# A gate table built in pipelined steps of four tokens, with projection weights split ahead and pick indices stored in pairs

## The chip, the core and the metric

The kernel runs on one core of one Trainium2 chip. A core has five engines that run at the same time: TensorE (PE in the profile; its weight loads are PEld), VectorE (DVE), ScalarE (ACT), GpSimd (POOL) and SyncE (SP, which issues DMA transfers). The metric is the device time of one execution in microseconds, the median of several runs.

## What is computed

The reference is one decoder block on 1024 tokens of width 1024: a mixing sub-layer (a short convolution beside windowed attention) and a retrieval of experts. In the retrieval each token has 8 heads; each head scores 128 "a" keys and 128 "b" keys, keeps the 16 best of each, adds them pairwise, keeps the 16 best sums and so names 16 of 16384 experts:

```python
q = (ht @ wq).reshape(t, PEER_HEADS, 2, PEER_DK)
va, ia = lax.top_k(sa, PEER_TOPK)
vb, ib = lax.top_k(sb, PEER_TOPK)
...
top, pos = lax.top_k(cand, PEER_TOPK)
eidx = jnp.take_along_axis(cidx, pos, axis=-1)
g = jax.nn.softmax(top, axis=-1).astype(ht.dtype)
a = jax.nn.gelu(jnp.einsum('thkd,td->thk', u, ht))
return jnp.einsum('thk,thkd->td', g * a, v)
```

## The kernel before

**Stages.** Three "fronts" treat 384, 384 and 256 tokens. A front does 18 input projections (`w_in`), attention and convolution, 8 output projections (`w_out`), and 16 query projections (`wq`) whose scores go through a first top 16. By the instructions of lines 342 to 560 in the trace, the first front runs to about 343 us, the second from 343 to 729, the third from 729 to 1023. Then `dense` follows: every expert against tokens 0 to 639, on TensorE, to the end. Tokens 640 to 1023 fetch their experts by indirect DMA beside it.

**Projections.** `proj` multiplies one 128-column block of weights in two half chunks of 4 x 128 rows. For a half chunk SyncE loads `wraw`, ScalarE makes `wH` (L268), GpSimd makes the remainder `wL` (L269, 128x512, both inputs in SBUF), and TensorE runs 12 matmuls (L272).

**The gate table.** The dense stage needs, for each token, a 128x128 table with the gate g at (ia, ib). For a block of 128 tokens `select` (L593 to L671) picks the 128 (ia, ib, g) triples of each token, and `spread` (L683 to L717) turns them around with three transposes, so that a token's 128 triples lie on the 128 partitions, and builds one table per token as a matmul of two one-hot matrices: `oi`, a row of g at column ia, and `oj`, a row of 1 at column ib. It works in steps of four tokens. The four `oi` of a step are made one by one, by the letters of `HOT = "APVV"`: one by ScalarE in two activations (L703, L704), one by GpSimd and two by VectorE (L706, a compare with `iota` times g, 128x128). VectorE makes `oj` for all four at once (L711, 128x512, two inputs in SBUF). TensorE does four matmuls into one PSUM tile `gps` (L714), ScalarE copies it out (L715), and a DMA writes 32 tokens' tables to `gd`. Five blocks (tokens 0 to 639) go through `spread`: 160 steps.

**Order.** `select` and `spread` are generators. They advance in `bg`, which `proj` calls once at its start with a credit that comes to about 4 steps for 384 tokens and 3 for 256. So blocks 0 to 2 are spread within the second front and blocks 3 and 4 within the third. The framework's scheduler then orders each engine's instructions; an engine runs its own queue strictly in that order, and semaphores hold an instruction until its inputs and its buffer are free.

**Picking.** In `select`, L660 makes a one-hot over 16 ranks (128x2048, bf16), L662 multiplies it by the candidates' indices `idf`, which are broadcast along the innermost dimension, and L666 and L668 add up.

Of the kernel before, what the change touches and what calls it, by code (L numbers as in the profile page):

```python
# [47 lines left out]
GT = 3  # L48
J = 4
TB = 32  # L50
HOT = "APVV"
RATE0, RATE = 0.0, 0.49
ORDER = True
BACK = 0
# [20 lines left out]
def hymba_peer_kernel(ctx: ExitStack, tc: tile.TileContext, a, out: bass.AP):  # L75
# [181 lines left out]
    def ch(t, c):  # L257
        return t[c // 4][:, c % 4, :]

    def proj(wsrc, sH, sL, T):  # L260
        bg(24 * T / 2400 + 0.5)
        pt = pj.tile([P, TM], F32, name="pj")
        for h in range(2):
            w = wp.tile([P, 4, P], F32, name="wraw")
            nc.sync.dma_start(w, wsrc[:, 4 * h:4 * h + 4, :])
            wH = wp.tile([P, 4, P], F32R, name="wH")
            wL = wp.tile([P, 4, P], F32R, name="wL")
            A.copy(wH, w)  # L268
            G.tensor_tensor(wL, w, wH.bitcast(F32), op=ALU.subtract)  # L269
# [62 lines left out]
    def front(t0, T, hs, nxt):  # L332
# [9 lines left out]
        A.copy(kc, proj(a["w_in"][4], hH, hL, T))  # L342
        qT = [tmp("y", bufs=4)[:, 0:T] for c in range(4)]
        for c in range(4):
            A.copy(qT[c], proj(a["w_in"][c], hH, hL, T))
        vT = tmp("q")
        A.copy(vT[:, 0:T], proj(a["w_in"][5], hH, hL, T))

        def conv():
            ys = []  # L350
            for cc in range(4):
                cs = tmp("q")[:, 0:T]
                A.copy(cs, proj(a["w_in"][6 + 3 * cc], hH, hL, T))
# [3 lines left out]
                V.tensor_tensor(u[:, 2:T + 2], cs, proj(a["w_in"][7 + 3 * cc], hH, hL, T), op=ALU.mult)  # L357
# [6 lines left out]
                V.tensor_tensor(y, y, proj(a["w_in"][8 + 3 * cc], hH, hL, T), op=ALU.mult)  # L364
# [191 lines left out]
        for mm in range(0, 16, 2):  # L556
            qs = []
            for m in (mm, mm + 1):
                qq = tmp("q")[:, 0:T]
                A.copy(qq, proj(a["wq"][m], h2H, h2L, T))  # L560
# [30 lines left out]
            V.max_index(u[:, 8:16], v[:, 8:16], s)  # L591

    def select(va, iu):  # L593
        idf = sel.tile([P, 2 * PH, 16], BF16, name="idf")
        A.copy(idf, iu)
        va4 = va.rearrange("p (h s) k -> p h s k", s=2)
        id4 = idf.rearrange("p (h s) k -> p h s k", s=2)
        cand = sel.tile([P, PH, NCAND], F32, name="cand")
# [7 lines left out]
        pairs(1, 3, 8, 16)  # L606
        pairs(4, 4, 4, 40)
        pairs(8, 8, 1, 56)
        top = sel.tile([P, PH, 16], F32, name="top")
        pu = sel.tile([P, PH, 16], U32, name="pu")  # L610
        yield
        for m0 in range(0, 8, 4):
# [44 lines left out]
        for s, src in ((0, aab), (1, stb)):  # L657
            r = ft(f"pick{s}", tag=("a3", "st3")[s])
            hot1 = sel.tile([P, PH, 16, 16], BF16, name="hot1")
            V.tensor_tensor(hot1, src.rearrange("p (h k) -> p h k", h=PH).unsqueeze(2).to_broadcast([P, PH, 16, 16]),  # L660
                            rank.unsqueeze(1).to_broadcast([P, PH, 16, 16]), op=ALU.is_equal)
            V.tensor_tensor(hot1, hot1, id4[:, :, s, :].unsqueeze(3).to_broadcast([P, PH, 16, 16]), op=ALU.mult)  # L662
            yield
            m = 8
            while m > 1:
                V.tensor_tensor(hot1[:, :, 0:m, :], hot1[:, :, 0:m, :], hot1[:, :, m:2 * m, :], op=ALU.add)  # L666
                m //= 2
            V.tensor_tensor(r.rearrange("p (h k) -> p h k", h=PH), hot1[:, :, 0, :], hot1[:, :, 1, :], op=ALU.add)  # L668
            yield
            res.append(r)  # L670
# [10 lines left out]
        V.tensor_copy(gate[:, ti, :], g)  # L681

    def spread(ti, ia, ib, g):  # L683
        gb = env["gb"]
        pat = HOT
# [3 lines left out]
        tr = gb.tile([P, 3, P], F32, name="tr", bufs=2)  # L689
        A.copy(tr, tps)  # L690
        ng = gb.tile([P, 2, P], F32, name="ng", bufs=1)
        A.activation(ng, tps[:, 0:3:2, :], AF.Copy, scale=-1.0)
        for q in range(P // TB):
            stage = gat.tile([P, P, TB], F32, name="stage")
            for t4 in range(0, TB, 4):
                ps = gp.tile([P, 4, P], F32, name="gps")
                ois = []
                for x in range(4):
                    t = q * TB + t4 + x
                    oi = gb.tile([P, P], F32, name="oi", bufs=6)  # L700
                    who = pat[t % len(pat)]
# [6 lines left out]
                    ois.append(oi)  # L708
                t = q * TB + t4
                oj = gb.tile([P, 4, P], F32, name="oj", bufs=2)  # L710
                V.tensor_tensor(oj, iota.unsqueeze(1).to_broadcast([P, 4, P]),  # L711
                                tr[:, 1, t:t + 4].unsqueeze(2).to_broadcast([P, 4, P]), op=ALU.is_equal)
                for x in range(4):
                    PE.matmul(ps[:, x, :], ois[x], oj[:, x, :], start=True, stop=True)  # L714
                A.copy(stage[:, :, t4:t4 + 4], ps.rearrange("p t j -> p j t"))  # L715
                yield
            nc.sync.dma_start(gd[(ti * P - DT0) // TB + q], stage)  # L717

    def gather():
        state = {"n": 0}  # L720
# [299 lines left out]
    with tc.tile_pool(name="ada", bufs=2, side="right") as ap:  # L1020
# [109 lines left out]
```

## Time and profile before

| | us |
|---|---|
| median of 3 runs | 2851.67 (2851.33 to 2851.88) |
| the profiled execution | 2857.49 |
| its span, first to last instruction | 2855.7 |
| VectorE busy in the span | 2373.4 (83%) |
| TensorE busy | 2700.5 (95%) |
| GpSimd busy | 1721.7 (60%) |
| ScalarE busy | 1093.9 (38%) |

The shares are means over stages that differ. The time of a stage is read from the rows of that stage. A busy TensorE is not TensorE at its peak, since its matmuls overlap.

### The profile page before, as it was taken

The page shows a single profiled execution, that of the slowest core. Times are in us where ns is not written, and L with a number is a line of the kernel's source. Part 1 is how long each engine was busy: PE and PEld are TensorE (multiplying, and loading weights), DVE is VectorE, ACT ScalarE, POOL GpSimd, SP SyncE. Part 2 cuts the span into 40 slices and gives each one's busy share as a digit, 9 for nine tenths or more (in the row PEclk, how much of TensorE's full clock was granted, in tenths as well). Part 3 has the DMA queues.
Part 4 walks back from the last instruction along what each step waited for, and adds up shares of the span by engine and source line. Part 5 has one row for each costly group of instructions (what it writes and reads, how often), then busy time and mean ns, then how long its engine had stood idle before and what let it go on. Part 6 is the DMA issues. An engine that isn't in the chain of part 4 may idle for free.

```text
span 2855.7 us, 45148 instructions
## 1 busy us (share of the span) xinstructions
PE 2700.5 (95%) x15679; PEld 2445.9 (86%) x15679; DVE 2373.4 (83%) x4845; ACT 1093.9 (38%) x2193; POOL 1721.7 (60%) x1491
## 2 busy tenths in 40 slices
PE   8899988999787889999999999999999999999998
PEld 6788978789786778889989989999989889988987
DVE  3665898877899697888988888888889888888887
ACT  2455468775586643222322222232222222222221
POOL 3444475656667744666666666666666666666661
PEclk7999999999999989999999999999999999999999
DMA  7647423464344677999999999999999999999995
GB/s 243 217 155 232 121 103 115 158 216 156 97 151 137 234 227 229 342 337 343 326 322 346 340 344 335 349 325 332 347 334 324 325 339 346 333 336 345 324 327 193
DMA packets 345157, 764.31 MB, mean 268 GB/s; under 512 B 31296, under 2 KB 130016, under 8 KB 341984
## 3 DMA queue, kind: packets, MB, share of 16 engines
q0 software_dynamic: 112320, 408.99, 39.6%
q1 hardware_dynamic: 231168, 349.81, 37.4%
q8 instruction: 123, 2.02, 0.3%
q10 hardware_dynamic: 1440, 2.62, 0.2%
q14 instruction: 106, 0.87, 0.1%
HBM read 702.06 MB, written 59.24 MB: 267 GB/s over the span
## 4 chain that ended last, share of the span: by engine, by line
PE 44%; DMA 8%; DVE 6%; issue 5%; POOL 2%; ACT 1%; SPq 0%; DVEq 0%; POOLq 0%; ACTq 0%
PE pv L873 22%; PE pa L816 21%; DMA vraw<-in_v 4%; DMA uraw<-in_uT 2%; DVE pq L768 2%; DVE vdL L860 1%; POOL rows L741 1%; ACT vdH L859 1%; DVE rows L760 1%; DMA wraw<-in_wq 1%; DMA rows<-in_v,eidx 1%; POOL uL L800 1%; DVE dacc L892 0%; DVE gw L835 0%; PE pj L272 0%
## 5 line engine op out<-in xcount | busy, mean ns | idle before, releaser
L816 PE MATMUL pa<-h,uH 128*128 128x320 f32 x4096 | 772.9, 311 | 15.2 <-ACT uH L799 6.2
L816 PEld LDWEIGHTS pa<-h,uH 128*128 128x128 f32 x4096 | 648.8, 189 | 23.1 <-ACT uH L799 7.2
L873 PE MATMUL pv<-vdH,wdH 128*128 128x512 f32 x1275 | 500.0, 392 | 18.0 <-DVE dacc L892 16.4
L269 POOL TENSOR_TENSOR wL<-wraw,wH 128x512 fp32r<-128x512 f32 x252 | 351.5, 1402 | 272.7 <-ACT wH L268 249.4
L873 PE MATMUL pv<-vdL,wdH 128*128 128x512 f32 x1275 | 497.8, 390 | 0.1
L873 PE MATMUL pv<-vdH,wdL 128*128 128x512 f32 x1275 | 496.8, 390 | 0.0
L816 PE MATMUL pa<-h,uL 128*128 128x320 f32 x2048 | 469.2, 310 | 2.3 <-POOL uL L800 2.3
L800 POOL TENSOR_TENSOR uL<-uraw,uH 128x512 fp32r<-128x512 f32 x256 | 342.4, 1338 | 163.3 <-ACT uH L799 142.7
L741 POOL DMA_INDIRECT rows<-in_u,eidx x257 | 260.8, 1015 | 157.1 <-DVE aw L760 83.2
L741 POOL DMA_INDIRECT rows<-in_v,eidx x254 | 253.7, 999 | 164.6 <-DVE pq L768 117.1
L816 PEld LDWEIGHTS pa<-h,uL 128*128 128x128 f32 x2048 | 344.6, 189 | 3.3 <-POOL uL L800 3.3
L768 DVE SCALAR_TENSOR_TENSOR pq<-rows,aw,pq 128x1024 f32<-128x1024 f32 x253 | 324.5, 1282 | 3.3 <-DMA rows<-in_v,eidx 0.8
L892 DVE TENSOR_TENSOR dacc<-dacc,pv 128x512 f32<-128x512 f32 x310 | 211.9, 684 | 134.0 <-PE pv L873 111.4
L859 ACT CAST vdH<-vraw 128x512 fp32r<-128x512 f32 x255 | 153.5, 619 | 439.0 <-DMA vraw<-in_v 366.4
L799 ACT CAST uH<-uraw 128x512 fp32r<-128x512 f32 x256 | 158.3, 619 | 418.9 <-DMA uraw<-in_uT 340.5
L760 DVE CUSTOM_DVE_ANT_0 rows<-rows,pq 128x1024 f32<-128x1024 f32 x257 | 307.5, 1212 | 12.5 <-DMA rows<-in_u,eidx 10.9
L873 PEld LDWEIGHTS pv<-vdH,wdH 128*128 128x128 f32 x1275 | 239.6, 188 | 74.9 <-DVE dacc L892 24.7
L873 PEld LDWEIGHTS pv<-vdH,wdL 128*128 128x128 f32 x1275 | 239.8, 188 | 50.9
L873 PEld LDWEIGHTS pv<-vdL,wdH 128*128 128x128 f32 x1275 | 239.8, 188 | 47.3 <-DVE vdL L860 0.5
L706 POOL TENSOR_SCALAR oi<-iota,tr 128x128 f32<-128x128 f32 x160 | 198.5, 1243 | 96.2 <-PE gps L714 88.1
L860 DVE TENSOR_TENSOR vdL<-vraw,vdH 128x512 fp32r<-128x512 f32 x255 | 192.1, 770 | 71.7 <-ACT vdH L859 66.7
L842 ACT CAST wdH<-gw 128x640 fp32r<-128x640 f32 x128 | 93.0, 728 | 377.0 <-DVE gw L835 342.4
(257 smaller groups left out, 5085.7 us busy)
## 6 DMA issues: line engine op xcount, KB each, us to landing
uraw<-in_uT SPq DMA_DIRECT2D x256, 256.0 KB
vraw<-in_v SPq DMA_DIRECT2D x255, 256.0 KB
gd<-stage SPq DMA_DIRECT2D x20, 2048.0 KB
gt<-gd SPq DMA_DIRECT2D x160, 256.0 KB
wraw<-in_w_in SPq DMA_DIRECT2D x108, 256.0 KB
wraw<-in_wq SPq DMA_DIRECT2D x96, 256.0 KB
wt<-in_w_ada SPq DMA_DIRECT2D x40, 512.0 KB
wraw<-in_w_out SPq DMA_DIRECT2D x48, 256.0 KB
```

The source lines that it names most:

```text
L269: G.tensor_tensor(wL, w, wH.bitcast(F32), op=ALU.subtract)
L706: (G if who == "P" else V).tensor_scalar(oi, iota, tr[:, 0, t:t + 1], tr[:, 2, t:t + 1], op0=ALU.is_equal, op1=ALU.mult)
L741: G.indirect_dma_start(out=r, out_offset=None, in_=table, in_offset=bass.IndirectOffsetOnAxis(ap=eidx[:, ti, k:k + 1], axis=0))
L760: V.tensor_tensor_reduce(out=r, in0=r, in1=h2, op0=ALU.mult, op1=ALU.add, scale=1.0, scalar=0.0, accum_out=aw[:, k:k + 1])
L768: V.scalar_tensor_tensor(acc, r, aw[:, k:k + 1], acc, op0=ALU.mult, op1=ALU.add)
L799: A.copy(uH, raw)
L800: G.tensor_tensor(uL, raw, uH.bitcast(F32), op=ALU.subtract)
L816: PE.matmul(AT[j][:, s, 0:n], l[:, c, :], h2[r][4 * h + c][:, s * n:s * n + n], start=(h == 0 and c == 0 and k == 0), stop=(h == 1 and c = ...
L859: A.copy(vH, raw)
L860: V.tensor_tensor(vL, raw, vH.bitcast(F32), op=ALU.subtract)
L873: PE.matmul(pt, l[:, P * tt:P * tt + P], r, start=(m == 0), stop=(m == 3 * J - 1))
L892: V.tensor_tensor(dst, dst, pt, op=ALU.add)
```

## The change

It does four things.

1. `spread` becomes a pipeline. A step is still four tokens, but the four `oi` are made together, by two instructions: VectorE compares a table of `iota` repeated four times with the four ia (`hots`, 128x512, bf16), and GpSimd multiplies that by the four g (`oi`, 128x512). One call of the generator makes `hots` for step k+2, `oi` and `oj` for step k+1, the matmuls of step k, and the copy-out of step k-1. `oi` has 2 buffers of four tokens. ScalarE's two activations and the 128x128 compares on VectorE and GpSimd are gone.
2. `split` loads and splits a half chunk of weights one half chunk before `proj` multiplies it, in a fixed list of all projections.
3. `proj` calls `bg` twice, once per half chunk, with half the credit each.
4. `idf` holds each index twice, side by side, so that the product of L662 (now L678) is read in pairs. `cand` shares its buffer with `hot1`, `top` with `bits`.

```diff
+    def split():
+        nm, m, h = coming.pop(0)
+        w = wp.tile([P, 4, P], F32, name="wraw")
+        nc.sync.dma_start(w, a[nm][m][:, 4 * h:4 * h + 4, :])
...
+        A.copy(wH, w)
+        G.tensor_tensor(wL, w, wH.bitcast(F32), op=ALU.subtract)
+        ready.append(((nm, m, h), wH, wL))
-    def proj(wsrc, sH, sL, T):
-        bg(24 * T / 2400 + 0.5)
+    def proj(name, m, sH, sL, T):
         for h in range(2):
...
+            key, wH, wL = ready.pop(0)
+            if coming:
+                split()
+            bg(12 * T / 2400 + 0.25)
...
-            V.tensor_tensor(hot1, hot1, id4[:, :, s, :].unsqueeze(3).to_broadcast([P, PH, 16, 16]), op=ALU.mult)
+            hk = hot1.rearrange("p h a (k y) -> p (h a) k y", y=2)
+            V.tensor_tensor(hk, hk, idf[:, s].unsqueeze(2).to_broadcast([P, PH * 16, 8, 2]), op=ALU.mult)
...
-                    if who == "A":
-                        A.activation(oi, iota, AF.Abs, bias=ng[:, 0, t:t + 1])
-                        A.activation(oi, oi, AF.Relu, scale=ng[:, 1, t:t + 1], bias=tr[:, 2, t:t + 1])
-                    else:
-                        (G if who == "P" else V).tensor_scalar(oi, iota, tr[:, 0, t:t + 1], tr[:, 2, t:t + 1],
-                                                               op0=ALU.is_equal, op1=ALU.mult)
...
+        def hot(k):
+            hots[k] = gb.tile([P, P, 4], BF16, name="hots", bufs=2)
+            V.tensor_tensor(hots[k], iotas, tri[:, 4 * k:4 * k + 4].unsqueeze(1).to_broadcast([P, P, 4]),
+                            op=ALU.is_equal)
+        def pair(k):
+            oi = ois[k] = gb.tile([P, 4, P], F32, name="oi", bufs=2)
+            G.tensor_tensor(oi, hots.pop(k).rearrange("p i x -> p x i"),
+                            tr[:, 1, 4 * k:4 * k + 4].unsqueeze(2).to_broadcast([P, 4, P]), op=ALU.mult)
+            oj = ojs[k] = gb.tile([P, 4, P], F32, name="oj", bufs=2)
+            V.tensor_tensor(oj, iota.unsqueeze(1).to_broadcast([P, 4, P]),
+                            tr[:, 0, 4 * k:4 * k + 4].unsqueeze(2).to_broadcast([P, 4, P]), op=ALU.is_equal)
...
+        for k in range(-2, n + 1):
+            for step, d in ((hot, 2), (pair, 1), (table, 0), (evict, -1)):
+                if 0 <= k + d < n:
+                    step(k + d)
```

VectorE's queue where the first table steps of the second front stand, before (`pu`, `cand` and `top` belong to the next block's `select`, `grs` to the attention's norm):

```order
L711 TENSOR_TENSOR oj<-iota,tr 128x512 x2
L706 TENSOR_SCALAR oi<-iota,tr 128x128 x2
L585 MAX_INDEX pu<-top,cand 128x8
L587 MATCH_REPLACE cand<-top,cand 128x64
L706 TENSOR_SCALAR oi<-iota,tr 128x128 x2
L587 MATCH_REPLACE cand<-top,cand 128x64
L711 TENSOR_TENSOR oj<-iota,tr 128x512
```

and after, at the same place:

```order
L714 TENSOR_TENSOR hots<-iotas,tri 128x512 x2
L722 TENSOR_TENSOR oj<-iota,tr 128x512
L714 TENSOR_TENSOR hots<-iotas,tri 128x512
L722 TENSOR_TENSOR oj<-iota,tr 128x512
L714 TENSOR_TENSOR hots<-iotas,tri 128x512
L596 MAX top<-cand 128x8
L722 TENSOR_TENSOR oj<-iota,tr 128x512
```

A step now has two VectorE instructions where it had three, and both of them read two tensors from SBUF.

GpSimd's queue in the second front's input projections, before:

```order
L269 TENSOR_TENSOR wL<-wraw,wH 128x512 x3
L706 TENSOR_SCALAR oi<-iota,tr 128x128 x6
L269 TENSOR_TENSOR wL<-wraw,wH 128x512
L706 TENSOR_SCALAR oi<-iota,tr 128x128 x2
L269 TENSOR_TENSOR wL<-wraw,wH 128x512
```

and after:

```order
L272 TENSOR_TENSOR wL<-wraw,wH 128x512 x4
L719 TENSOR_TENSOR oi<-hots,tr 128x512 x8
L272 TENSOR_TENSOR wL<-wraw,wH 128x512
L719 TENSOR_TENSOR oi<-hots,tr 128x512 x4
L272 TENSOR_TENSOR wL<-wraw,wH 128x512 x5
```

There is still one GpSimd instruction per step, but it has become a TENSOR_TENSOR of 128x512, of the kind of `wL`.

## Rows read from the trace of the kernel before

**Rows 1.** Windows: length, busy us by PE, PEld, DVE, ACT, POOL, clock, DMA.
```profile
59.00:343.00 284.00, 265.60 (x1476) 237.99 (x1476) 183.84 (x584) 134.58 (x297) 128.50 (x94) 0.96 0.59 188
377.00:548.00 171.00, 152.35 (x1009) 133.25 (x1007) 159.27 (x468) 134.68 (x335) 113.43 (x90) 0.99 0.33 119
548.00:729.00 181.00, 172.78 (x1089) 161.57 (x1089) 134.68 (x514) 112.30 (x251) 111.85 (x89) 0.99 0.54 182
757.00:960.00 203.00, 168.61 (x1222) 150.16 (x1221) 184.07 (x499) 146.67 (x352) 145.23 (x113) 0.97 0.42 149
960.00:1023.00 63.00, 57.73 (x473) 55.62 (x471) 38.64 (x226) 32.39 (x75) 45.08 (x37) 1.00 0.62 200
1140.00:2855.00 1715.00, 1690.93 (x9431) 1534.43 (x9429) 1489.24 (x1932) 448.89 (x728) 1068.75 (x989) 1.00 0.94 330
```
**Rows 2.** DVE groups by shape, 377 to 548 us: busy us, mean ns | idle before.
```profile
L706 DVE TENSOR_SCALAR oi<-iota,tr 128x128 f32<-128x128 f32 x114 | 44.6, 430 | 6.4 <-PE gps L714 6.1
L711 DVE TENSOR_TENSOR oj<-iota,tr 128x512 f32<-128x512 f32 x57 | 42.7, 768 | 1.4 <-PE gps L714 1.3
```
**Rows 3.** POOL groups by shape, 377 to 548 us.
```profile
L269 POOL TENSOR_TENSOR wL<-wraw,wH 128x512 fp32r<-128x512 f32 x24 | 33.3, 1390 | 20.2 <-ACT wH L268 17.1 <-DVE gsum L620 1.8 <-DVE st L648 0.7
```
**Rows 4.** DVE groups by shape, 757 to 960 us.
```profile
L711 DVE TENSOR_TENSOR oj<-iota,tr 128x512 f32<-128x512 f32 x61 | 48.6, 814 | 1.6 <-ACT tr L690 1.2 <-issue 0.2
L706 DVE TENSOR_SCALAR oi<-iota,tr 128x128 f32<-128x128 f32 x120 | 44.8, 410 | 8.7 <-PE gps L714 8.4
L662 DVE TENSOR_TENSOR hot<-hot,idf 128x2048 bf16<-128x2048 bf16 x5 | 14.2, 2838 | 0.0
```
**Rows 5.** POOL groups by shape, 757 to 960 us.
```profile
L269 POOL TENSOR_TENSOR wL<-wraw,wH 128x512 fp32r<-128x512 f32 x41 | 60.1, 1472 | 19.3 <-ACT wH L268 18.9
```
**Rows 6.** Single lines, whole span: ns min/median/max, first and last start us, forms.
```profile
L711 DVE TENSOR_TENSOR oj<-iota,tr x160: 637/683/1793, 377.3 to 967.0; 128x512 f32<-128x512 f32 x160
...
L706 DVE TENSOR_SCALAR oi<-iota,tr x320: 240/340/1379, 378.5 to 968.8; 128x128 f32<-128x128 f32 x160
L706 POOL TENSOR_SCALAR oi<-iota,tr x160: 783/1230/2813, 377.4 to 968.8; 128x128 f32<-128x128 f32 x160
...
L269 POOL TENSOR_TENSOR wL<-wraw,wH x252: 1258/1292/6322, 51.9 to 1019.3; 128x512 fp32r<-128x512 f32 x126
...
L662 DVE TENSOR_TENSOR hot<-hot,idf x16: 2265/2283/3369, 362.8 to 1091.6; 128x2048 bf16<-128x2048 bf16 x16
...
L660 DVE TENSOR_TENSOR hot<-stb,rank x8: 1200/1210/2317, 369.4 to 1088.2; 128x2048 bf16<-128x2048 bf16 x8
...
L666 DVE TENSOR_TENSOR hot<-hot x48: 267/413/2042, 366.3 to 1098.8; 128x1024 bf16<-128x1024 bf16 x16, 128x512 bf16<-128x512 bf16 x16, 128x256 bf16<-128x256 bf16 x16
```
**Rows 7.** Timeline, DVE, about 420 and 562 us: start us, us, instruction.
```profile
420.24 2.37 DVE L711 TENSOR_TENSOR oj<-iota,tr 128x512 f32<-128x512 f32 x2
...
562.51 0.59 DVE L706 TENSOR_SCALAR oi<-iota,tr 128x128 f32<-128x128 f32 x2
563.03 0.68 DVE L711 TENSOR_TENSOR oj<-iota,tr 128x512 f32<-128x512 f32 x1
563.63 0.74 DVE L706 TENSOR_SCALAR oi<-iota,tr 128x128 f32<-128x128 f32 x2
564.20 0.68 DVE L711 TENSOR_TENSOR oj<-iota,tr 128x512 f32<-128x512 f32 x1
```
**Rows 8.** Timeline, POOL, about 420 and 562 us.
```profile
420.53 1.53 POOL L269 TENSOR_TENSOR wL<-wraw,wH 128x512 fp32r<-128x512 f32 x1
...
562.80 2.83 POOL L706 TENSOR_SCALAR oi<-iota,tr 128x128 f32<-128x128 f32 x2 [0.54 <-PE gps L714]
```
**Rows 9.** Waits of PE, 59 to 343 us: us in total, times, longest.
```profile
PE pj L272 <- ACT wH L268: 2.8, 1, 2.8
PE pj L272 <- POOL wL L269: 2.5, 5, 0.7
```

More of the change, by code (lines that the diff above doesn't have):

```diff
@@ L50 @@
 TB = 32
-HOT = "APVV"
 RATE0, RATE = 0.0, 0.49
@@ L258, in ch @@
         return t[c // 4][:, c % 4, :]
-    def proj(wsrc, sH, sL, T):
-        bg(24 * T / 2400 + 0.5)
+    coming = [(nm, m, h) for _ in GROUPS
+              for nm, ms in (("w_in", (4, 0, 1, 2, 3, 5, *range(6, 18))), ("w_out", range(8)), ("wq", range(16)))
+              for m in ms for h in range(2)]
+    ready = []
+    def split():
+        nm, m, h = coming.pop(0)
+        w = wp.tile([P, 4, P], F32, name="wraw")
+        nc.sync.dma_start(w, a[nm][m][:, 4 * h:4 * h + 4, :])
+        wH = wp.tile([P, 4, P], F32R, name="wH")
+        wL = wp.tile([P, 4, P], F32R, name="wL")
+        A.copy(wH, w)
+        G.tensor_tensor(wL, w, wH.bitcast(F32), op=ALU.subtract)
+        ready.append(((nm, m, h), wH, wL))
+    def proj(name, m, sH, sL, T):
         pt = pj.tile([P, TM], F32, name="pj")
         for h in range(2):
[L264 to L269, printed above, removed]
+            key, wH, wL = ready.pop(0)
+            assert key == (name, m, h)
+            if coming:
+                split()
+            bg(12 * T / 2400 + 0.25)
             for c in range(4):
@@ L341, in front @@
         kc = tmp("k", bufs=1)[:, 0:T]
-        A.copy(kc, proj(a["w_in"][4], hH, hL, T))
+        A.copy(kc, proj("w_in", 4, hH, hL, T))
         qT = [tmp("y", bufs=4)[:, 0:T] for c in range(4)]
         for c in range(4):
-            A.copy(qT[c], proj(a["w_in"][c], hH, hL, T))
+            A.copy(qT[c], proj("w_in", c, hH, hL, T))
         vT = tmp("q")
-        A.copy(vT[:, 0:T], proj(a["w_in"][5], hH, hL, T))
+        A.copy(vT[:, 0:T], proj("w_in", 5, hH, hL, T))
         def conv():
@@ L352, in conv @@
                 cs = tmp("q")[:, 0:T]
-                A.copy(cs, proj(a["w_in"][6 + 3 * cc], hH, hL, T))
+                A.copy(cs, proj("w_in", 6 + 3 * cc, hH, hL, T))
                 yield
@@ L559, in front @@
                 qq = tmp("q")[:, 0:T]
-                A.copy(qq, proj(a["wq"][m], h2H, h2L, T))
+                A.copy(qq, proj("wq", m, h2H, h2L, T))
                 qs.append(qq)
@@ L593, in select @@
     def select(va, iu):
-        idf = sel.tile([P, 2 * PH, 16], BF16, name="idf")
-        A.copy(idf, iu)
+        idf = sel.tile([P, 2, PH * 16, 2], BF16, name="idf")
+        iu4 = iu.rearrange("p (h s) a -> p h s a", s=2)
+        for s in range(2):
+            A.copy(idf[:, s].rearrange("p (h a) y -> p h a y", h=PH),
+                   iu4[:, :, s, :].unsqueeze(3).to_broadcast([P, PH, 16, 2]))
         va4 = va.rearrange("p (h s) k -> p h s k", s=2)
-        id4 = idf.rearrange("p (h s) k -> p h s k", s=2)
-        cand = sel.tile([P, PH, NCAND], F32, name="cand")
+        cand = sel.tile([P, PH, NCAND], F32, name="cand", tag="hot1")
         def pairs(a0, na, nbb, st):
@@ L608, in select @@
         pairs(8, 8, 1, 56)
-        top = sel.tile([P, PH, 16], F32, name="top")
+        top = sel.tile([P, PH, 16], F32, name="top", tag="bits", bufs=2)
         pu = sel.tile([P, PH, 16], U32, name="pu")
@@ L683, in spread @@
     def spread(ti, ia, ib, g):
-        gb = env["gb"]
-        pat = HOT
+        gb, iotas = env["gb"], env["iotas"]
         tps = gp.tile([P, 3, P], F32, name="gps")
@@ L688, in spread @@
             PE.transpose(tps[:, k, :], src, ident)
[L689 to L701, printed above, removed]
-                    if who == "A":
-                        A.activation(oi, iota, AF.Abs, bias=ng[:, 0, t:t + 1])
-                        A.activation(oi, oi, AF.Relu, scale=ng[:, 1, t:t + 1], bias=tr[:, 2, t:t + 1])
-                    else:
-                        (G if who == "P" else V).tensor_scalar(oi, iota, tr[:, 0, t:t + 1], tr[:, 2, t:t + 1],
-                                                               op0=ALU.is_equal, op1=ALU.mult)
[L708 to L715, printed above, removed]
@@ new lines, in spread @@
+        tri = gb.tile([P, P], BF16, name="tri", bufs=2)
+        A.copy(tri, tps[:, 0, :])
+        tr = gb.tile([P, 2, P], F32, name="tr", bufs=2)
+        A.copy(tr, tps[:, 1:3, :])
+        n, per = P // 4, TB // 4
+        hots, ois, ojs, outs, stages = {}, {}, {}, {}, {}
+        def hot(k):
+            hots[k] = gb.tile([P, P, 4], BF16, name="hots", bufs=2)
+            V.tensor_tensor(hots[k], iotas, tri[:, 4 * k:4 * k + 4].unsqueeze(1).to_broadcast([P, P, 4]),
+                            op=ALU.is_equal)
@@ new lines, in table, with evict @@
+        def table(k):
+            ps = outs[k] = gp.tile([P, 4, P], F32, name="gps")
+            oi, oj = ois.pop(k), ojs.pop(k)
+            for x in range(4):
+                PE.matmul(ps[:, x, :], oi[:, x, :], oj[:, x, :], start=True, stop=True)
+        def evict(k):
+            q, r = divmod(k, per)
+            if r == 0:
+                stages[q] = gat.tile([P, P, TB], F32, name="stage")
+            A.copy(stages[q][:, :, 4 * r:4 * r + 4], outs.pop(k).rearrange("p t j -> p j t"))
+            if r == per - 1:
+                nc.sync.dma_start(gd[(ti * P - DT0) // TB + q], stages.pop(q))
@@ L716, in spread @@
+        for k in range(-2, n + 1):
+            for step, d in ((hot, 2), (pair, 1), (table, 0), (evict, -1)):
+                if 0 <= k + d < n:
+                    step(k + d)
+            if 0 <= k < n:
                 yield
-            nc.sync.dma_start(gd[(ti * P - DT0) // TB + q], stage)
     def gather():
@@ L1040, in hymba_peer_kernel @@
             pass
+        split()
         hs = norm1(*GROUPS[0], x0c)
@@ L1048, in hymba_peer_kernel @@
     env["gb"] = gbc.__enter__()
+    env["iotas"] = env["gb"].tile([P, P, 4], BF16, name="iotas")
+    A.copy(env["iotas"], iota.unsqueeze(2).to_broadcast([P, P, 4]))
     for (t0, T), nxt in zip(GROUPS[1:], nxts[1:]):
```

6 lines of the change are left out of this document (3 added, 3 removed).

## The prediction

> **What bounds the kernel now.** I read the windows first, since the page's shares are means over unlike stages. The dense stage from 1140 us on has TensorE busy for 1690.9 of 1715 us [rows 1]. The change doesn't touch it, so whatever the change is worth lies in the fronts. There the table steps run in three stretches. In the second front's input projections, 377 to 548 us, VectorE is busy for 159.3 of 171 us, TensorE for 152.4. In the third front's input and output projections, 757 to 960, it is 184.1 of 203 against 168.6 [rows 1]. In both VectorE has the least idle time. In 548 to 729, where the second front's output and query projections stand, it is the other way round: TensorE 172.8 of 181, VectorE 134.7. So of the 160 steps [rows 6] the 57 of the first stretch and the 61 of the second, counted by `oj` [rows 2, 4], run where VectorE sets the pace. A microsecond given to or taken from VectorE counts there, while the other 42 steps are mostly covered by matmuls.
>
> Next I asked what VectorE's busy time is made of, since a busy row can hide a wait. An `oj` takes 0.683 us in the median [rows 6], but 0.768 on average in the first stretch and 0.814 in the second [rows 2, 4]. An `oi` takes 0.340 in the median and 0.430 and 0.410 on average. The timeline shows why. At 420.24 two `oj` take 2.37 us [rows 7]. GpSimd's `wL` was started at 420.53, inside the first, and ended at 422.06 [rows 8]. The first `oj`, of 0.68 us, ended at 420.92, so `wL` ended 1.14 us after it, and the second `oj` ended 0.55 us after `wL`. The two engines took turns: a two-input GpSimd instruction holds VectorE's two-input instruction back for 1.14 us, and the other way round. GpSimd's `oi`, a TENSOR_SCALAR, does nothing like it. At 562.80 two of them are spread over 2.83 us, where one takes 0.783 at its shortest [rows 6, 8], while VectorE goes on beside them: `oi` pair, `oj`, `oi` pair, `oj` start 0.52, 0.60 and 0.57 us apart [rows 7]. GpSimd's part of a step is slow, and VectorE does not pay for it.
>
> **The change part by part.** The sum is over the 118 steps in the two stretches and is laid on the median of 2851.67. The profiled execution, whose rows I use, took 2857.49, 0.2% more (span 2855.7); differences of tens of microseconds carry over.
>
> *VectorE's own work.* Before, a step costs it 0.52 for two `oi` and 0.60 for `oj`, 1.12 us from start to start [rows 7]. After, it costs `hots` and `oj`. For `hots` (128x512, two bf16 inputs) the nearest row is the addition of L666, whose middle third is 128x512: median 0.41 [rows 6]; less the 0.08 by which `oj`'s spacing is under its duration, 0.33. With `oj` that is 0.93, or -0.19 per step: -22 us. Bounds: with `hots` as slow as `oj` +9; with the 0.27 of L666's shortest, which is half as wide, -39.
>
> *The pick product.* L662 takes 2.28 us; L660, of the same shape with its innermost run contiguous, 1.21 [rows 6]. There are two per block, six blocks fall in the fronts: 12 x -1.07 = -13, bounds 0 and -13. The other four products lie at the start of the dense stage beside other work: -2, bounds 0 and -4. The Trainium skill ("Vector Engine (DVE) Microarchitecture Reference", "Measured stream behaviour on trn2") says that a port streams at full rate only over runs of at least two adjacent 4-byte words; a pair of bf16 is one such word. By its figures (1.73 against 1.05 ns per column) the product would stay near 2 us, -4 in place of -13 and a time of 2879, as an estimate; no row here shows it.
>
> *GpSimd's product, the term that decides.* `oi` becomes a two-input TENSOR_TENSOR of 128x512. The trace has no such GpSimd instruction with a bf16, strided input; the nearest row is `wL`, 1.29 us in the median, of which 1.14 stand in VectorE's way. How much of that VectorE really loses is p, between 0 (the product always meets VectorE idle or in one-input work) and 1.14 (never). The nearest rows are again `wL`: in the first stretch VectorE's `oj` and `oi` are stretched by 57 x 0.085 + 114 x 0.09 = 15.1 us against 24 `wL`, 0.63 each [rows 2, 3]; in the second by 61 x 0.131 + 120 x 0.07, and L662 by 5 x 0.555, 19.2 us against 41 `wL`, 0.47 each [rows 4, 5]. I take 0.65, at the upper of these: the product of step k+1 is released by the matmuls of step k-1, and the same matmuls release `oj` of step k+1, so that the two come out together. 118 x 0.65 = +77 us; ends 0 and +135. GpSimd itself has room: 113 of 171 and 145 of 203 us busy [rows 1]. Behind a held product stands the next `wL` on its queue, for which the matmuls of the next half chunk wait; behind a held `hots` stands `oj`.
>
> *Waits that the pipeline takes away.* VectorE waits for the tables' PSUM and `oi` buffers, 6.1 and 8.4 us [rows 2, 4]. With everything made a step ahead I take 13 of these 14.5 back. TensorE's idle time in 548 to 729 is 8.2 us [rows 1]; some of it is for tables: -3, bounds 0 and -8. What is late next is VectorE, not TensorE.
>
> *Split ahead.* It pays where TensorE waits for weights and sets the pace: 2.8 and 2.5 us in the first front [rows 9], and part of the 5.3 idle us of the third front's query projections, 960 to 1023 [rows 1]: -6 in all, bounds 0 and -10. In the two stretches it only moves waits behind VectorE. Its DMA issues go out earlier on SyncE's queue and wait for the same three buffers.
>
> *Costed at nothing:* ScalarE loses two activations per step; it is 79% and 72% busy in the stretches, so it is nowhere the pace, and what others waited for it is counted above. The repeated `iota`, the second copy of `idf` and the shared buffers lie on it too, or behind VectorE's own order. Dealing twice leaves the number of steps per projection as it was; if it makes the load more even, that is in p.
>
> Sum: -22 - 13 - 2 + 77 - 13 - 3 - 6 = +18 us, **2870**.
>
> **The rivals.** Without the product's hold the rest comes to -59, so p = 0.50 is where the change turns from loss to gain; a measurement of this kernel tells 0.2%, 5.7 us, from nothing, which is p outside 0.45 to 0.55.
>
> *The product falls into gaps (faster).* Place: GpSimd in the two stretches. The maxima of `select` and the instructions that read PSUM stand between the table steps, and GpSimd may run a step ahead. With p = 0.25: +30 - 59 = -29, 2823. For it: 0.47 in the second stretch. Against it: a buffer of two steps cannot choose its moment.
>
> *GpSimd stood in the way all along (faster).* If the old `oi` already stood in VectorE's way for its 0.78 us, the new product only adds 1.14 - 0.78 = 0.36 of hold: p = 0.65 x 0.36 / 1.14 = 0.21, +24 - 59 = -35, 2817. The row at 562.80 speaks against it. The Trainium skill ("SBUF — State Buffer", "SBUF: two separate sides") has it so: the shared port pair goes to whichever starts first, for the whole instruction, and the other fully blocks. For `wL` the trace agrees (1.14 and 0.55); for GpSimd's one-input `oi` it does not.
>
> *Nothing to be seen.* p of 0.45 to 0.55: within 5.7 us of 2852. The edits cancel.
>
> *The product is slower than `wL` (slower still).* It gathers bf16 four elements apart. At 1.9 us, holding 1.75, p is 0.57 x 1.75 = 1.0: +118 - 59 = +59, 2911. Nothing in the trace speaks for or against.
>
> **How the numbers follow.** The hold as worked out: 0.42, from 2857 to 2900 (its own range). Gaps: 0.26. In the way all along: 0.08. Nothing: 0.14. Slower product: 0.10. So faster 0.34, same 0.14, slower 0.52, and the prediction is the likeliest case, 2870. The ends of the bounds are 2763 (p = 0 and all gains at their most) and 2996 (p = 1.14, `hots` at its slowest, no gain); both need every unknown on one side. Cutting the outer parts of the two faster cases and of the slower product, about 0.15 in all, leaves 2812 to 2918.
>
> **What the profile after would show.** If I am right, the tables' waits on TensorE are nearly gone, ScalarE is freed, the 512-wide `oj` on VectorE is stretched more than now (a mean of 1 us or above in the stretch of the second front's input projections, `hots` likewise, against a lowest value of 0.4), GpSimd's product takes 1.3 us or more, and the second and third fronts end later, by some 20 us together. The term for L662 is right if its line shows about 1.2 us. I am wrong if `oj` keeps its mean of 0.77 to 0.81 beside the products, or if the product is well under 1.29 us; then the fronts end earlier than 729 and 1023 us.

## The result, and the profile after

| | before | after |
|---|---|---|
| median, us | 2851.78 (4 runs) | 2985.55 (4 runs, 2983.12 to 2991.99) |
| ratio, 95% interval | 1 | 1.0469 (1.0449 to 1.0488) |
| profiled execution, us | 2857.49 | 2985.44 |

The change makes the kernel 134 us slower, where 18 were forecast. The direction was right, and so was the hold that the prediction named; the size was far off and lies outside the range given. The profiled executions, from which the rows below are read, differ by 128 us.

The dense stage is as long as before (the 1715 us that begin at 1265 hold 1696.2 us of TensorE, where [rows 1] had 1690.9). The loss lies in the second and third front: 126 of the 128 us. Cut at the first matmul of each group of projections, with the table steps counted by their matmuls (1280 records for 160 steps, rounded; before, the stages had 56, 24, 16, 37, 19 and 8 steps):

| stage | before, us | after, us | steps after | loss per step |
|---|---|---|---|---|
| second front, input projections | 209.9 | 257.2 | 58 | 0.82 |
| output projections | 72.3 | 90.6 | 22 | 0.83 |
| query projections | 106.7 | 118.0 | 17 | 0.66 |
| third front, input projections | 161.3 | 187.0 | 36 | 0.71 |
| output projections | 62.4 | 80.2 | 22 | 0.81 |
| query projections | 73.4 | 78.5 | 6 | 0.85 |

Every stage loses 0.66 to 0.85 us per step, those too in which the prediction had put the steps under the cover of matmuls. The windows of the changed kernel at these cuts (the first row is the first front; columns as in [rows 1]):

```profile
47.00:337.30 290.30, 272.95 (x1466) 239.73 (x1466) 186.24 (x550) 138.38 (x302) 138.08 (x99) 0.93 0.57 185
337.30:594.50 257.20, 198.91 (x1174) 177.25 (x1173) 225.98 (x608) 112.45 (x257) 140.94 (x103) 0.90 0.30 105
594.50:685.10 90.60, 72.65 (x421) 65.17 (x420) 51.42 (x58) 32.30 (x62) 52.52 (x41) 0.92 0.35 118
685.10:803.10 118.00, 107.32 (x633) 103.23 (x631) 92.97 (x380) 52.12 (x110) 60.89 (x46) 0.91 0.49 166
803.10:990.10 187.00, 143.31 (x925) 129.68 (x924) 163.34 (x513) 86.25 (x204) 107.13 (x80) 0.86 0.33 110
990.10:1070.30 80.20, 60.62 (x401) 56.12 (x402) 67.63 (x78) 26.19 (x52) 57.62 (x43) 0.85 0.46 158
```

In no stage is one engine full: in the second front's output projections (third row) TensorE is busy for 73 of 90.6 us, VectorE for 51, GpSimd for 53. The engines wait for one another in turn. The granted clock of TensorE, 0.95 to 1.00 in the same stages before, is 0.85 to 0.92 in the five shown (rows two to six). The lines of the step, ns min/median/max:

```profile
L714 DVE TENSOR_TENSOR hots<-iotas,tri x160: 401/1246/3676, 373.2 to 1089.4; 128x512 bf16<-128x512 bf16 x160
L722 DVE TENSOR_TENSOR oj<-iota,tr x160: 623/693/1786, 373.8 to 1092.3; 128x512 f32<-128x512 f32 x160
L719 POOL TENSOR_TENSOR oi<-hots,tr x160: 1036/1329/2021, 373.7 to 1091.8; 128x512 f32<-128x512 bf16 x160
L678 DVE TENSOR_TENSOR hot<-hot,idf x16: 1214/1224/2297, 358.3 to 1225.3; 128x2048 bf16<-128x2048 bf16 x16
```

`hots` takes three times its shortest, 0.40, in the median. GpSimd's product takes 1.33 us, hardly more than `wL` (1.30 in the same trace). And the groups of the two VectorE instructions from 330 us to the end of the fronts (busy, mean | idle before them):

```profile
L722 DVE TENSOR_TENSOR oj<-iota,tr 128x512 f32<-128x512 f32 x160 | 165.0, 1034 | 31.4 <-PE gps L729 30.9 <-ACT tr L708 0.2
L714 DVE TENSOR_TENSOR hots<-iotas,tri 128x512 bf16<-128x512 bf16 x160 | 149.2, 939 | 46.9 <-POOL oi L719 39.9 <-ACT tri L706 7.0
```

The same view of the kernel before:

```profile
L706 DVE TENSOR_SCALAR oi<-iota,tr 128x128 f32<-128x128 f32 x320 | 123.5, 424 | 22.9 <-PE gps L714 21.5
L711 DVE TENSOR_TENSOR oj<-iota,tr 128x512 f32<-128x512 f32 x160 | 122.4, 783 | 4.7 <-PE gps L714 2.8 <-ACT tr L690 1.4 <-issue 0.2
```

VectorE is busy with them for 314.2 us, where it was 245.9. It is idle ahead of them for 78.3 us against 27.6. TensorE's waits in the two fronts (us in total, times, longest) say who is late:

```profile
PE gps L729 <- DVE oj L722: 75.6, 53, 4.5
PE pj L285 <- POOL wL L272: 16.5, 12, 4.6
PE gps L729 <- ACT stage L735: 12.4, 13, 2.8
PE gps L729 <- POOL oi L719: 10.6, 13, 3.3
```

Before, the tables' wait for `oj` was:

```profile
PE gps L714 <- DVE oj L711: 8.5, 12, 1.5
```

It has risen from 8.5 to 75.6 us. The timeline of a burst shows why (start, us, instruction [idle before]):

```profile
467.17 0.68 DVE L722 TENSOR_TENSOR oj<-iota,tr 128x512 f32<-128x512 f32 x1
467.42 1.33 POOL L719 TENSOR_TENSOR oi<-hots,tr 128x512 f32<-128x512 bf16 x1 [0.45 <-PE gps L729]
467.77 1.26 DVE L714 TENSOR_TENSOR hots<-iotas,tri 128x512 bf16<-128x512 bf16 x1
...
467.99 1.13 PE L729 MATMUL gps<-oj,oi 128*128 128x128 f32 x8 [0.66 <-ACT stage L735]
468.95 0.68 DVE L722 TENSOR_TENSOR oj<-iota,tr 128x512 f32<-128x512 f32 x1
...
469.20 1.32 POOL L719 TENSOR_TENSOR oi<-hots,tr 128x512 f32<-128x512 bf16 x1 [0.46 <-PE gps L729]
...
469.77 0.46 PE L729 MATMUL gps<-oj,oi 128*128 128x128 f32 x2 [0.65 <-ACT stage L735]
```

The product ends at 468.75 and `hots`, begun 0.98 us earlier, ends 0.28 us after it; `oj` stands behind `hots` on VectorE's queue and ends at 469.63; 0.14 us later the matmuls of its step start (their row names the copy-out that ended 0.02 us before, but `gps` has two buffers, and the one that these matmuls write was copied out by 467.96). A step takes 1.78 us, where `oj` to `oj` was 1.17 in [rows 7]. Two readings fit this burst; a third looks for the harm outside the steps. **Theory A, hold:** product and VectorE's two-input instructions take turns, 0.28 + 0.60 for `hots` and `oj`, then 0.89 until the next product ends. **Theory B, ring:** product k+2 waits for the `oi` buffer that the matmuls of step k free, and they wait for an `oj` that stands behind product k; product 1.32, rest of `hots` 0.29, `oj` 0.60, 0.14, matmuls 1.13, 0.08 come to 3.56 us for two steps. **Theory C:** splitting ahead and dealing twice do the harm.

### The profile page after: what moved, and what is told of

Its sections match the earlier page's. It is cut to its first block, busy times and chain, and to the rows that moved or that the text cites. A ratio compares the mean times of both kernels' runs of the same rounds, so it can differ in the third digit from the quotient of the medians.

```text
span 2983.7 us, 44869 instructions
## 1 busy us (share of the span) xinstructions
PE 2755.3 (92%) x15679; PEld 2500.4 (84%) x15679; DVE 2435.1 (82%) x4685; ACT 986.1 (33%) x1880; POOL 1739.1 (58%) x1491
## 4 chain that ended last, share of the span: by engine, by line
PE 47%; DVE 6%; DMA 5%; issue 5%; POOL 2%; ACT 1%; SPq 0%; POOLq 0%; DVEq 0%; ACTq 0%
PE pv L900 23%; PE pa L843 22%; DMA vraw<-in_v 4%; DVE pq L795 1%; DVE vdL L887 1%; PE pj L285 1%; POOL rows L768 1%; DMA uraw<-in_uT 1%; DVE rows L787 1%; PE gps L729 1%; DVE oj L722 1%; DMA wraw<-in_wq 1%; POOL uL L827 0%; POOL wL L272 0%; DVE dacc L919 0%
## 5 line engine op out<-in xcount | busy, mean ns | idle before, releaser
L272 POOL TENSOR_TENSOR wL<-wraw,wH 128x512 fp32r<-128x512 f32 x252 | 359.1, 1432 | 299.6 <-ACT wH L271 266.9
L729 PE MATMUL gps<-oj,oi 128*128 128x128 f32 x1280 | 219.2, 317 | 103.4 <-DVE oj L722 75.6
L719 POOL TENSOR_TENSOR oi<-hots,tr 128x512 f32<-128x512 bf16 x160 | 209.8, 1322 | 172.0 <-PE gps L729 148.4
L729 PEld LDWEIGHTS gps<-oj,oi 128*128 128x128 f32 x1280 | 197.2, 225 | 129.1 <-POOL oi L719 51.1
```

The costliest lines, as they stand in the source:

```text
L719: G.tensor_tensor(oi, hots.pop(k).rearrange("p i x -> p x i"), tr[:, 1, 4 * k:4 * k + 4].unsqueeze(2).to_broadcast([P, 4, P]), op=ALU.mult)
L729: PE.matmul(ps[:, x, :], oi[:, x, :], oj[:, x, :], start=True, stop=True)
```

## The experiments

The kernel before was timed again beside each group of runs, on the chip of that group: 2856.63 for the first four runs, then 2855.39, 2855.82, 2857.15 and 2857.58. The result's own was 2851.78, so a difference between two groups is good to some 5 us.

**The old steps put back, and the new steps alone.** The first is the changed kernel with `spread` of before, of which this is one line:

```diff
-            G.tensor_tensor(oi, hots.pop(k)..., tr[:, 1, ...], op=ALU.mult)
+            (G if who == "P" else V).tensor_scalar(oi, iota, tr[:, 0, t:t + 1], tr[:, 2, t:t + 1], ...)
```

> The changed kernel with the old table steps (four separate compares, one of four on GpSimd) put back; weights split ahead, steps dealt twice and pick indices in pairs stay. Theory A (port: GpSimd's two-input product holds VectorE's two-input instructions) and theory B (loop: two buffers of oi and oj tie product, hots, oj and tables into a ring) both put the whole loss into the new steps, so that the rest is worth what the prediction gave it, -15 for the pairs and -6 for the split: 2825 to 2845 us. Theory C (splitting ahead puts wL in the way on GpSimd's queue, or dealing twice harms): most of the loss stays, 2900 or more.

2856.36 us, ratio 1.0003 (0.9990 to 1.0016).

> The kernel before with the new table steps alone (old projections, old pick product; cand and top share buffers as in the change, for room). Theories A and B: all of the loss and none of the small gains, 2985 + 15 + 6, so 2990 to 3010 us. Theory C: 2850 to 2900.

2975.87 us, 1.0414 (1.0391 to 1.0438). The new steps alone cost 119 us, and without them nothing is lost: theory C falls. Both runs missed their ranges. The second stayed 14 us under 2990, and the first did not come down to 2845: the small gains did not come.

**A copy in place of the product.**

```diff
-            G.tensor_tensor(oi, hots.pop(k).rearrange("p i x -> p x i"), tr[...], op=ALU.mult)
+            G.tensor_copy(oi, hots.pop(k).rearrange("p i x -> p x i"))
```

> The changed kernel with GpSimd's product replaced by a GpSimd copy of the same shape from hots to oi: one input in place of two, the same buffers and waits. The gates are left out of the tables, so the output is not the reference's. Theory A: hots and oj go back to about 0.40 and 0.68 us, and the hold, 0.89 us a step over 160 steps, goes: 2985 - 142, so 2830 to 2870. Theory B: the ring loses only what the copy is shorter than 1.32 us; at 1.0 us that is 0.16 a step, 2950 to 2975, and nothing if the copy is as long.

2904.68 us, 1.0176 (1.0155 to 1.0198), between the two. The groups of VectorE show that the hold became smaller and did not go:

```profile
L721 DVE TENSOR_TENSOR oj<-iota,tr 128x512 f32<-128x512 f32 x160 | 154.3, 968 | 27.9 <-PE gps L728 27.2 <-ACT tr L708 0.2
L714 DVE TENSOR_TENSOR hots<-iotas,tri 128x512 bf16<-128x512 bf16 x160 | 115.5, 730 | 29.9 <-POOL oi L719 25.1 <-ACT tri L706 4.5
```

and its timeline, that a copy with one input holds VectorE too:

```profile
604.37 1.76 POOL L719 CAST oi<-hots 128x512 f32<-128x512 bf16 x2 [1.01 <-PE gps L728]
605.57 0.85 DVE L714 TENSOR_TENSOR hots<-iotas,tri 128x512 bf16<-128x512 bf16 x1 [0.53 <-POOL oi L719]
```

`hots` takes 0.85 there, 0.41 alone. VectorE's two groups are busy for 269.8 us, between the 314.2 of the change and the 215.9 of a later run without GpSimd in the steps. So this run took about half of the hold away, not all, and shortened the chain as well.

**`oj` ahead of `hots`.**

```diff
-            for step, d in ((hot, 2), (pair, 1), (table, 0), (evict, -1)):
+            for step, d in ((pair, 1), (hot, 2), (table, 0), (evict, -1)):
```

> The changed kernel with oi and oj of step k+1 written ahead of hots of step k+2, so that oj no longer stands behind hots on VectorE's queue. Theory A: the port serialises the same three instructions, 1.78 us a step in the bursts: 2970 to 3000. Theory B: the ring product, hots, oj, tables loses the 0.29 us of hots that lie in it, 0.15 a step: 2955 to 2965, and more if hots' wait for its buffer goes too.

2970.52 us, 1.0408 (1.0383 to 1.0432): 15 us less than the change. The interval is 7 us to either side and the two ranges lie 5 us apart, so this run decides nothing.

**Three buffers.**

```diff
-            oi = ois[k] = gb.tile([P, 4, P], F32, name="oi", bufs=2)
+            oi = ois[k] = gb.tile([P, 4, P], F32, name="oi", bufs=3)
```

and the same for `oj`; `x`, `tr` and `tri` have one buffer fewer.

> The changed kernel with three buffers each for oi and oj in place of two (paid for by one buffer fewer of x and single ones of tr and tri). Theory A (port): the two engines still take turns, product after oj, so the 1.78 us a step of the bursts stay: 2965 to 2985. Theory B (ring of two buffers): the ring of 3.56 us then holds three steps, 1.19 a step where it was 1.78; over 160 steps with two thirds of them in bursts that is 60 to 95 us: 2890 to 2925.

2958.10 us, 1.0363 (1.0329 to 1.0396): 27 us less, 7 below what theory A gave and 33 above theory B. The burst decides between them:

```profile
449.11 1.37 POOL L719 TENSOR_TENSOR oi<-hots,tr 128x512 f32<-128x512 bf16 x1 [0.42 <-DVE hots L714]
...
450.69 0.68 DVE L722 TENSOR_TENSOR oj<-iota,tr 128x512 f32<-128x512 f32 x1
450.90 1.37 POOL L719 TENSOR_TENSOR oi<-hots,tr 128x512 f32<-128x512 bf16 x1 [0.43 <-DVE hots L714]
...
451.29 1.28 DVE L714 TENSOR_TENSOR hots<-iotas,tri 128x512 bf16<-128x512 bf16 x1
452.49 0.68 DVE L722 TENSOR_TENSOR oj<-iota,tr 128x512 f32<-128x512 f32 x1
452.71 1.36 POOL L719 TENSOR_TENSOR oi<-hots,tr 128x512 f32<-128x512 bf16 x1 [0.43 <-DVE hots L714]
```

With room for three steps, products still start 1.79 and 1.81 us apart, and none waits for a matmul: each waits for `hots`, which takes 1.27 us instead of 0.41 and ends some 0.3 us after the product before. In the burst it is the hold. Where the 27 us came from was not followed; TensorE's waits for `oj` fell from 75.6 to 42.0 us.

**Both together.**

> The one-input copy of the earlier run and three buffers together (gates left out of the tables, so the output is not the reference's). The earlier run with the copy and two buffers took 2905, 49 us above the kernel before. If what was left there is the ring, it goes now: 2850 to 2865. If it is GpSimd's and VectorE's own work, or wL behind the copies, it stays: 2890 to 2910.

2897.92 us, 1.0140 (1.0114 to 1.0166): 7 us less than with the copy alone, which intervals of 6 and 7 us to either side do not tell from nothing. By the two ranges given, what the copy left is not the ring.

**An unread GpSimd instruction in the kernel before: two runs that tell nothing of the hold.**

```diff
-HOT = "APVV"
+HOT = "AVVV"
+                G.tensor_copy(env["junk"], iota.unsqueeze(1).to_broadcast([P, 4, P]))
```

> The kernel before with GpSimd's oi given to VectorE (HOT is AVVV) and in its place, once per step, a GpSimd copy of 128x512 from iota into a tile that nobody reads; it waits for nothing and nothing waits for it. The control of the next run. One more compare of 0.26 us a step on VectorE: +31 over the 118 steps, 2870 to 2890, by either theory.

2924.83 us, 1.0234 (1.0208 to 1.0260), 35 us above its range.

> As the run before, but the unread GpSimd instruction has two inputs, iota times a constant, 128x512, as wL and the new oi have. Theory A (port): each holds VectorE for 0.6 to 0.9 us, 160 times, 95 to 140 us over the run with the copy. Theory B (ring): nobody waits for it, and it falls into GpSimd's free time: within 10 us of the run with the copy.

3028.79 us, 1.0596 (1.0567 to 1.0624). The 104 us between them look like theory A. They are not: by the row of `junk`, these instructions read constants alone and the scheduler moved them up, to start at 234 us, in the first front, long before most tables. Copy, then product:

```profile
L713 POOL COPY junk<-iota x160: 605/614/947, 234.2 to 388.4; 128x512 f32<-128x512 f32 x160
```

```profile
L713 POOL TENSOR_TENSOR junk<-iota,onesd x160: 1252/1277/1686, 234.2 to 495.2; 128x512 f32<-128x512 f32 x160
```

There they stand ahead of `wL` on GpSimd's queue: 160 x (1.28 - 0.61) = 107 us is GpSimd's own time. The first front's query projections, 83 us before, take 130 us with the copy and 222 with the product. Nothing follows for the hold.

**The product on ScalarE, without GpSimd.**

```diff
+                A.activation(oi[:, x, :], hk[:, :, x], AF.Copy, scale=tr[:, 1, 4 * k + x:4 * k + x + 1])
```

for each of the four tokens, in place of the product.

> The changed kernel with the product by g done by ScalarE, four 128x128 activations a step scaled by g, and GpSimd left out of the table steps. Theory A (GpSimd's product and also its copy hold VectorE: hots took 1.26 us beside a product, 0.86 beside a copy, 0.41 alone): by a line through the runs with product (2985) and copy (2905) at 0.85 and 0.45 us of hold a step, no hold is 2815; ScalarE gets 1.6 us a step more and stays inside the old stretches (94.9 + 57.5 x 1.6 = 187 of 210 us): 2815 to 2870. Theory B (ring): the ring product, hots, oj, table of 3.56 us becomes 1.6 + 0.14 + 1.13 + 0.08 and what of oj lies in it, about 3.0: 2935 to 2950.

2880.80 us, 1.0097 (1.0063 to 1.0131): 105 us less than the change, beyond theory B, 11 short of theory A's range. VectorE's groups:

```profile
L723 DVE TENSOR_TENSOR oj<-iota,tr 128x512 f32<-128x512 f32 x160 | 140.9, 891 | 54.7 <-PE gps L730 54.0
L714 DVE TENSOR_TENSOR hots<-iotas,tri 128x512 bf16<-128x512 bf16 x160 | 75.0, 484 | 13.4 <-ACT oi L721 8.9 <-ACT tri L706 3.9
```

215.9 us busy. The product of the change adds 314.2 - 215.9 = 98 us to it, 0.61 per step. (The means are still above the 0.68 of the 112 `oj` and the 0.42 of the 135 `hots` that meet no GpSimd instruction; the 41 `oj` that meet only `wL` take 1.33 on average.)

**One token of four on GpSimd again.**

```diff
+                    G.tensor_scalar(oi[:, x, :], hk[:, :, x], tr[:, 1, 4 * k + x:4 * k + x + 1], None, op0=ALU.mult)
```

> As the run before, but one of the four tokens by a GpSimd TENSOR_SCALAR of 128x128 (of the kind that did not hold VectorE in the kernel before) and three by ScalarE. Theory A: no hold, and ScalarE has 0.4 us a step less to do: 2815 to 2860, at or below the run with four on ScalarE. If the TENSOR_SCALAR holds as the copy does, 0.1 us a step more: 2835 to 2885. Theory B: 2915 to 2945.

2878.50 us, 1.0074 (1.0046 to 1.0101). GpSimd's TENSOR_SCALAR reads `hots` too and does not hold VectorE: beside it alone `hots` takes 0.417 us in the median (74 times), beside nothing 0.414.

```profile
580.80 2.10 POOL L724 TENSOR_SCALAR oi<-hots,tr 128x128 f32<-128x128 bf16 x2 [0.70 <-PE gps L733]
582.08 0.42 DVE L714 TENSOR_TENSOR hots<-iotas,tri 128x512 bf16<-128x512 bf16 x1
```

**The small edits one by one**, on the kernel before: the `idf` of the change alone, then `split` and the two calls of `bg` per projection alone.

> The kernel before with the pick indices in pairs alone (the two shared buffers go with them). The prediction's term: -15, 2837. The rival, after the run with the old table steps came out at the time of before: VectorE's saved time lies where the next thing is late anyway, within 6 us of before.

2851.08 us, 0.9983 (0.9969 to 0.9997): -5.

> The kernel before with the weights split one half chunk ahead and the steps dealt twice, alone. The prediction's term: -6, 2846. The rival: wL comes ahead of the work that VectorE and GpSimd owe the tables and eats the gain of the pairs: +10 to +15, 2862 to 2867.

2862.07 us, 1.0020 (1.0005 to 1.0035): +6.

Both intervals reach some 4 us to either side.

**An unread product, pinned to its step.** The product of the change, beside ScalarE's, into a tile that nobody reads; it reads `hots`, so it can't move up.

```diff
+            G.tensor_tensor(junk, hk.rearrange("p i x -> p x i"), tr[...].to_broadcast([P, 4, P]), op=ALU.mult)
```

> The run with all four tokens on ScalarE (2881 us), and beside it GpSimd's product of hots and g as in the changed kernel, into a tile that nobody reads (bf16). It reads hots, so it runs at its step; hots has three buffers, and oi does not wait for it. Theory A (hold): 0.65 to 0.89 us a step come back, +104 to +142: 2985 to 3023 us; where it falls into gaps less, but 2940 at the least. Theory B (ring): nothing but the third hots behind it waits for it: 2870 to 2895.

2953.27 us, 1.0329 (1.0311 to 1.0346): +72 on the run without it, within the range that theory A left for gaps. No table waits for its result, so a ring through `oi` can't be the cause. But the hold is not the only cause left. VectorE's groups, and one of TensorE's waits:

```profile
L726 DVE TENSOR_TENSOR oj<-iota,tr 128x512 f32<-128x512 f32 x160 | 159.2, 1004 | 60.3 <-PE gps L733 59.7
L714 DVE TENSOR_TENSOR hots<-iotas,tri 128x512 bf16<-128x512 bf16 x160 | 95.9, 619 | 7.3 <-ACT oi L724 3.9 <-ACT tri L706 3.0
```

```profile
PE pj L285 <- POOL wL L272: 52.4, 37, 4.6
```

VectorE's two instructions are busy for 255.1 us, 39 more than the 215.9 without the product: 0.25 per product, less than in the change (this product writes bf16 and takes 1.10 us in the median). And TensorE waits for `wL` 52.4 us, where it was 22.9 without the product: the product takes GpSimd's time ahead of `wL`, as in the two runs with an unread instruction that read constants. In the change that wait is 16.5 us. So of the 72 us about 40 go with the hold and up to 30 with GpSimd's own queue. How the 105 us between the change and the product on ScalarE divide between the hold and the matmuls' waiting for the product's result is not shown; three buffers gave 27 back.

**What stays without a hold.** The same three buffers in the run with one token on GpSimd; then also `oj` first and the old projections; then two tokens each on ScalarE and GpSimd:

> The run with three tokens on ScalarE and one on GpSimd (2878 us), with three buffers each of oi and oj. If the 23 us left over are the ring of two buffers: 2848 to 2862. If they are ScalarE's pace or wL in the way: 2872 to 2885.

2883.32 us, 1.0087 (1.0070 to 1.0103).

> A try at a better version: the kernel before with the pairs and with the pipelined steps, the product dealt to ScalarE (three tokens) and GpSimd (one, TENSOR_SCALAR), three buffers of oi and oj, oj written ahead of hots; weights are not split ahead and steps are dealt once per projection. Without a hold VectorE has 0.19 us a step less to do than before, but ScalarE 0.3 more: 2835 to 2855 by theory A with B; 2865 or more if ScalarE sets the pace of the steps.

2885.47 us, 1.0104 (1.0087 to 1.0121).

> As the run before with two tokens on ScalarE and two on GpSimd: ScalarE has 0.1 us a step less than in the kernel before, GpSimd 0.6 to 1 more: 2830 to 2850 if ScalarE was the pace there; 2860 or more if GpSimd's slow TENSOR_SCALARs stand ahead of wL and hold the matmuls.

2931.89 us, 1.0247 (1.0216 to 1.0277). Neither ring nor split explains the 23 us that stay (all three runs have one buffer of `x`, `tr` and `tri` fewer, which may hide a small gain), and a second TENSOR_SCALAR on GpSimd costs 46 more. The last two keep the pipeline's order and make the four `oi` as before (one on ScalarE, one on GpSimd, two on VectorE), with and without the split:

```diff
+        for k in range(-1, n + 1):
+            for step, d in ((pair, 1), (table, 0), (evict, -1)):
```

> The changed kernel with the pipeline order kept (oi and oj of step k+1, matmuls of k, copy-out of k-1 in one call) but the four oi made as before (ScalarE one, GpSimd one, VectorE two, from iota; 8 buffers of one token). If the order costs the 23 us: 2875 to 2885. If the deal to ScalarE costs them: 2845 to 2860, beside the 2856 of the run with the old table steps.

2850.22 us, 0.9981 (0.9965 to 0.9998).

> The same without the split ahead and the double dealing, with the pairs: a last try at a better version. Beside the run with the pairs alone, 2851: 2838 to 2850 if the order takes away TensorE's waits for oi (14.3 + 6.3 us in the kernel before), 2865 to 2880 if the order costs.

2863.21 us, 1.0021 (1.0008 to 1.0034), 2 us short of the range in which the order costs. The order makes -6 us with the split (beside 2856.36, within the noise of the two) and +12 without it (beside 2851.08). With the split in both, the old deal under the same order has none of the 23 us, so they come with the new deal of the product. With all four tokens there, TensorE's two largest waits were:

```profile
PE gps L730 <- ACT stage L736: 28.6, 25, 2.7
PE pj L285 <- POOL wL L272: 22.9, 25, 4.6
```

the first of them 3.9 us in the kernel before. ScalarE's copy-out stands in a queue with four activations a step more; that this is the whole of the 23 us was argued and not tested. The best version, pipeline order with the old deal and the split, is 0.19% under before; the pairs alone are 0.17% under it. Both are at the edge of what can be measured.

## Why the prediction was wrong in size

**VectorE's own work, -0.19 per step: right.** Without the product, 215.9 against 245.9 us over 160 steps is -0.19. It bought no time there: that run took 25 us more than before, and its VectorE waited 68.1 us ahead of its step instructions, where it had been 27.6.

**The pick product, -13 and -2: duration right, worth wrong.** L678 takes 1.224 us, as read from L660; the pairs gave 5 us instead of 15. The prediction's estimate from the Trainium skill ("Vector Engine (DVE) Microarchitecture Reference", "Measured stream behaviour on trn2"), about 2 us for pairs of bf16, did not appear; it carried figures for 4-byte streams over to bf16.

**GpSimd's product: right per step, wrong in count.** 0.65 was taken for p; VectorE's rows give 0.61. But it was summed over 118 steps, on the ground that 42 are covered by matmuls. By the table of stages these lose about as much as the others. The reading, argued from the burst: a step there lies among matmuls that need its result, and a hold inside the chain to a matmul is not covered by the matmuls behind it. 98 us in place of 77.

**Waits that the pipeline takes away, -13: this step failed most.** "With everything made a step ahead I take 13 of these 14.5 back." VectorE's waits ahead of its step instructions rose by 51 us instead (78.3 less 27.6), TensorE's waits for `oj` from 8.5 to 75.6. A call that makes `hots` of k+2 and `oj` of k+1 is a step ahead only while buffers are free. With two, the product waits for the matmuls, the next `hots` for the product, and `oj` for `hots` in VectorE's queue, so the hold comes back as waiting on three engines. The prediction named the queue ("behind a held `hots` stands `oj`") and priced it at nothing. Its own signs tell the same: GpSimd's product came out at 1.33 us as named and `oj` was stretched (a mean of 0.95 us in the second front's input projections, where 1 or above was named), but the tables' waits on TensorE, which were to be nearly gone, became the largest, and the third front ends 127 us later instead of some 20.

**Split ahead, -6: wrong sign, +6.** In the changed kernel the first front starts 6.2 us earlier, at 47.0 in place of 53.2, and still ends 1.5 us later.

Added up as if they were separate, VectorE's busy time +68, its waits +51, pairs -5 and split +6 come to 120 of the 128 us. That is no proof, for the same stages divide otherwise on TensorE. The sums of its windows over the six stages of the table, before and after:

```profile
sum 686.00, PE 601.90 PEld 547.14 DVE 581.60 ACT 454.09 POOL 452.33; mean PE 100.32 PEld 91.19 DVE 96.93 ACT 75.68 POOL 75.39
sum 811.50, PE 651.37 PEld 596.02 DVE 648.45 ACT 345.49 POOL 467.80; mean PE 108.56 PEld 99.34 DVE 108.08 ACT 57.58 POOL 77.97
```

With the same matmuls, TensorE is idle for 160 us instead of 84 and busy for 651 instead of 602. Busy time is 1.08 times as long, and the granted clock over both fronts fell by the same factor, from 0.97 to 0.90. How much of the 50 us is a cause of the loss, and how much only fills the time in which the next operand is late, no run isolates.

Of the rivals, "the product is slower than `wL`" falls by its 1.33 us, where 1.9 was assumed; "stood in the way all along" falls by the TENSOR_SCALAR run; "falls into gaps" falls by the 0.61 per step, where 0.25 was assumed.

## What to carry to other kernels

Price a hold between engines where the held instruction stands in a chain, not by the share of busy time of the stage: count every step, and add what waits behind the held instruction on its queue. Here a pipeline with two buffers did not hide the hold, it handed it on; write down the ring (who frees which buffer for whom) before a saved wait is entered in a sum. An unread instruction is a fair probe only if it reads something of its step, its row must show where it ran, and the waits for what stands behind it on its own queue must be taken off.

## What the hardware showed unexpectedly

Which GpSimd instructions hold VectorE is not told by the number of their inputs. Beside a TENSOR_TENSOR of 128x512 `hots` took 1.26 us, beside a one-input copy of that size 0.85, beside a TENSOR_SCALAR of 128x128 that reads `hots` too 0.42, alone 0.41. No run has the TENSOR_SCALAR at the size of the other two, so the size may count beside the kind. The Trainium skill ("SBUF — State Buffer", "SBUF: two separate sides") has a GpSimd instruction that reads SBUF and a VectorE instruction with two SBUF inputs shut each other out from a shared pair of ports for a whole instruction. Product and copy here agree, the TENSOR_SCALAR does not.
